# Feature-major FFN tiles in pairs by Strassen's seven block products, on one core of a Trainium2 chip

## The chip, the cores and the metric

The kernel runs on one core of one Trainium2 chip. The metric is the device time of one execution in microseconds (us), lower is better. Three runs of the kernel before the change took 1806.98, 1807.10 and 1807.12 us; the median is 1807.1 us.

A core has five engines that run side by side, each through its own queue of instructions in order: TensorE (PE; its weight loads are shown apart as PEld), VectorE (DVE), ScalarE (ACT), GpSimd (POOL) and SyncE (SP, which here only starts DMAs). TensorE multiplies a stationary block of 128x128 weights with a moving block of up to 512 columns and adds the result up in PSUM (8 banks of 512 float32 for each of the 128 partitions). ACT and DVE take results out of PSUM into SBUF.

## The reference, cut to what matters

512 tokens of width 1024 pass through three blocks. Two are the layers of a transformer, each with attention and a gated feed-forward network:

```python
def swiglu(x, w_in, w_out):                     # w_in 1024 x 5632, w_out 2816 x 1024
    gate, up = jnp.split(x @ w_in, 2, axis=-1)
    return (jax.nn.silu(gate) * up) @ w_out
```

The third has a gated mixer and a feed-forward network with a squared ReLU:

```python
    f = rmsnorm(h, pre_ff_g[l]) @ w_ff1[l]      # 1024 x 4096
    f = jnp.square(jax.nn.relu(f)) @ w_ff2[l]   # 4096 x 1024
```

All is float32. The change touches only the products `x @ w_in` (twice) and `h @ w_ff1` (once).

## The kernel before, in words

**Products in three passes.** Each float32 operand is held as two parts, `hi` (the value as ACT writes it into the type fp32r) and `lo` (the rest, from a subtraction on DVE). A product is hi*hi + hi*lo + lo*hi, three matmuls into one PSUM region (`passes`, L244 to L247).

**Weights.** The list `specs` holds every weight tile of 128x1024 numbers in the order of use. `Weights.load` (L62) starts its DMA into one of 3 raw buffers; `_split` (L77) makes `whi` on ACT (L93) and `wlo` on DVE (L94) into one of 5 pairs of buffers. `done(i)` marks a tile as used up and calls `fill`, which lets the split of tile i+5 follow. So weights are ready up to five tiles ahead.

**The feature-major tiles.** `in_tiles` (L381) runs over the tiles of an input product. One tile is 128 output features for all 512 tokens: 8 blocks of the depth of 1024, each in three passes, so 24 matmuls of 512 columns into one PSUM bank. The first few tiles of a phase (`lead`, 4 or 5) run their first 256 tokens early, while the normalisation of the other tokens is still under way, and so take 24 matmuls of 256 columns for each half. `ffn` (L642) has 22 gate and 22 up tiles in turn: `evac` takes silu of the gate tile (L651) and multiplies the up tile into it (L656). The squared-ReLU phase has 32 tiles, evacuated by L1134 (ACT) and L1135 (DVE).

**The output product.** `out_phase` (L347) then takes the hidden tiles one after another. `splitter` (L634) makes their two parts, `sh` on ACT (L637) and `sl` on DVE (L638), and `Out.__call__` (L320) does 4 token tiles x 2 halves x 3 passes of 512 columns (L333) for each.

**What sets the order.** DMA starts on SP follow the program's order. For the other engines a planner places the instructions when the kernel is built: it goes through them by their place in the program, takes an instruction earlier when its engine is free in the planner's own reckoning and all its inputs and buffers are there, and fixes one order for each engine. A pool's memory can be taken by a later pool once the last reader of the old tiles is done. Semaphores are set by the framework.

Of the kernel before, what the change touches and what calls it, by code (L numbers as in the profile page):

```python
# [10 lines left out]
F32 = mybir.dt.float32  # L11
F32R = mybir.dt.float32r
AF = mybir.ActivationFunctionType
OP = mybir.AluOpType
# [38 lines left out]
class Weights:  # L53


    def __init__(self, nc, raw, pairs, specs, n_raw, n_pairs):
        self.nc, self.raw, self.pairs, self.specs = nc, raw, pairs, specs
        self.n_raw, self.n_pairs = n_raw, n_pairs
        self.loaded, self.split, self.released = 0, 0, 0
        self.r, self.p, self.extra = {}, {}, set()  # L60

    def load(self, parts=0):  # L62
# [11 lines left out]
            return lambda m: self.nc.sync.dma_start(part(v, m), part(src, m))  # L74
        self.nc.sync.dma_start(v, src)

    def _split(self, pool, steps=1, name=None):  # L77
        i = self.split
        while self.loaded <= i:
            self.load()  # L80
        _, (a, b), _ = self.specs[i]
        t = self.r.pop(i)
# [12 lines left out]

        step(range((steps + 1) // 2))
        self.p[i] = tuple(w[:, :a * b].rearrange("p (a b) -> p a b", a=a) for w in (hi, lo))
        self.split += 1
        rest = lambda: step(range((steps + 1) // 2, steps))
        return rest  # L100

    def ahead(self, pool, n, name=None):

        for _ in range(n):
            self.extra.add(self.split)
            self._split(pool, name=name)
        while self.loaded < min(self.split + self.n_raw, len(self.specs)):
            self.load()

    def fill(self, steps=0):  # L110
        end = len(self.specs)
        if steps:
            return self._split(self.pairs, steps)
        while self.split < min(self.released + self.n_pairs + len(self.extra), end):
            self._split(self.pairs)
        while self.loaded < min(self.split + self.n_raw, end):
            self.load()

    def get(self, i):
        return self.p[i]  # L120
# [10 lines left out]
def body(ctx, tc, ins, out, stop=None, dbg=None):  # L131
# [11 lines left out]
    specs, at = [], {}  # L143

    def spec(key, w, r0, nk, c0, n, pad=None):
        at[key] = len(specs)
# [16 lines left out]
    def ffn_specs(l):  # L163
        w = ins["ffn_w_in"][l]
        for f in range(22):
            spec(("fg", l, f), w, 0, 8, 128 * f, 128)
            spec(("fu", l, f), w, 0, 8, FF + 128 * f, 128)
        rows(("fo", l), ins["ffn_w_out"][l], 22)

    ffn_specs(0)  # L170
# [20 lines left out]
    for f in range(32):  # L191
        spec(("f1", f), ins["w_ff1_2"], 0, 8, 128 * f, 128)
    rows("f2", ins["w_ff2_2"], 32)


# [13 lines left out]
    W = Weights(nc, raw, pairs, specs, 3, 5)  # L209

    def load_x(t):
        nc.sync.dma_start(x[t], ins["x"][0, ts(t), :])
# [36 lines left out]
    def bank(*shape):  # L249
        return psum.tile([128, *(shape or (512,))], F32, name="ps")  # L250
# [127 lines left out]
                after(1)  # L378
        finish(3, o.banks[3])

    def in_tiles(keys, evac, lead=0, tails=()):  # L381


        def run(key, p, a, b):
            w = W.get(at[key])
            for k in range(KT):
                passes(p[:, a:b], w, (xh, xl), k == 0, k == KT - 1, (slice(None), k), (slice(None), k, slice(a, b)))

        early = [bank() for _ in keys[:lead]]
        for n, key in enumerate(keys[:lead]):  # L390
            run(key, early[n], 0, 256)
            if n < len(tails):
                for f in tails[n]:
                    f()
        for n, key in enumerate(keys):
            p = early[n] if n < lead else bank()
            run(key, p, 256 if n < lead else 0, 512)
            W.done(at[key])
            evac(n, p)

    def part_project(key, state, part):

# [230 lines left out]
    def splitter(pool, src):  # L633
# [5 lines left out]
            return hi, lo  # L639
        return operand  # L640

    def ffn(l, tails, finish, after):  # L642
        with tc.tile_pool(name="hs", bufs=TAIL[l]) as hs, tc.tile_pool(name="silu", bufs=2) as sp, \
             tc.tile_pool(name="h", bufs=6) as hp:
            h, gate = [], {}

            def evac(n, p):
                f = n // 2
                if n % 2 == 0:
                    gate[f] = sp.tile([128, S], F32, name="gate")  # L650
                    nc.scalar.activation(gate[f], p, AF.Silu)  # L651
                else:
                    if f % 4 == 0:
                        four = hp.tile([128, 4 * S], F32, name="h4")
                        h.extend(four[:, n * S:n * S + S] for n in range(4))
                    nc.vector.tensor_tensor(h[f], p, gate.pop(f), op=OP.mult)  # L656

            keys = [k for f in range(22) for k in (("fg", l, f), ("fu", l, f))]
            in_tiles(keys, evac, 4, tails)
# [471 lines left out]
    h = hp.tile([128, 32, S], F32, name="h2")  # L1131

    def evac_f1(n, p):
        nc.scalar.activation(h[:, n], p, AF.Relu)  # L1134
        nc.vector.tensor_tensor(h[:, n], h[:, n], h[:, n], op=OP.mult)  # L1135

    in_tiles([("f1", f) for f in range(32)], evac_f1, 5, [[], [lambda: after_mix(2)], [], [], [lambda: after_mix(3)]])
    nc.sync.dma_start(gb[:, 0], bcast(ins["post_ff_g_2"], D))

    def finish_ff(t, banks):  # L1140
# [3 lines left out]
    def last_tile(o, ks):  # L1144
# [19 lines left out]
        for k in ks:  # L1164
            o.done(k)

    out_phase(Out("f2", range(32), splitter(hs, [h[:, k] for k in range(32)])), finish_ff, lambda t: None, 4,
              last=last_tile)


# [21 lines left out]
```

## Time and profile before

| | |
|---|---|
| median of 3 runs | 1807.1 us |
| profiled execution | 1812.42 us, of which 1810.6 us from the first to the last instruction |
| TensorE matmul busy | 1773.8 us (98%), 9092 matmuls |
| VectorE busy | 905.7 us (50%) |
| ScalarE busy | 774.7 us (43%) |
| granted TensorE clock | 0.995 of full speed |

The profile is one execution. Busy matmuls overlap in the records (each stands with its whole passage through the array), so the pace of a stream is read from the starts of its matmuls or from the length of a stretch over its count, not from the mean duration of one. "L247" is line 247 of the kernel; names such as `ps<-xh,whi` are the tiles written and read.

### The profile page before, as it was taken

What the parts mean: (1) busy time and instruction counts of PE and PEld (TensorE: products, weight loads), DVE (VectorE), ACT (ScalarE), POOL (GpSimd) and SP (SyncE); (2) the same over time, 40 slices, a digit from 0 to 9 for tenths busy, and PEclk for the clock granted to TensorE, in tenths of its full rate; (3) what the DMA queues carried; (4) which work ended last, traced back from release to release, by engine and by line L of the source; (5) the groups of instructions that cost most, each with busy time, mean ns of one, the idle gap of its engine ahead of it and who ended that gap; (6) DMA issues with size and microseconds to landing.
All of it is one profiled execution on the core that took longest, in us unless ns stands there. A gap on an engine that the chain in (4) does not pass through costs nothing.

```text
span 1810.6 us, 23050 instructions
## 1 busy us (share of the span) xinstructions
PE 1773.8 (98%) x9092; PEld 1499.7 (83%) x9092; DVE 905.7 (50%) x1620; ACT 774.7 (43%) x1341; POOL 69.7 (4%) x125
## 2 busy tenths in 40 slices
PE   8899999999999989999999999999999999999998
PEld 8788788888888878888888888888877898888886
DVE  6888854323234557777633223346456553333333
ACT  6878833222223348878432222233434433223222
POOL 0000000000000020000000000001001100000000
PEclk9999999999999989999999999999999999999999
DMA  6122233333333172222333332342222243333231
GB/s 201 58 59 71 70 128 94 96 102 93 96 126 116 48 228 82 87 83 70 105 105 93 99 99 93 122 136 71 75 77 79 79 117 93 94 104 105 93 104 48
DMA packets 198221, 176.62 MB, mean 98 GB/s; under 512 B 7009, under 2 KB 175137, under 8 KB 198113
## 3 DMA queue, kind: packets, MB, share of 16 engines
q1 hardware_dynamic: 194384, 162.48, 29.5%
q0 software_dynamic: 3152, 10.84, 2.0%
q8 instruction: 71, 1.16, 0.3%
q10 hardware_dynamic: 576, 1.84, 0.3%
q14 instruction: 38, 0.30, 0.1%
HBM read 172.99 MB, written 7.38 MB: 100 GB/s over the span
## 4 chain that ended last, share of the span: by engine, by line
PE 88%; ACT 5%; DVE 4%; issue 1%; DMA 1%; POOL 0%; SPq 0%; DVEq 0%; POOLq 0%; ACTq 0%
PE ps L247 52%; PE ps L333 29%; PE ps L263 1%; PE ps L739 1%; PE ps L751 1%; ACT whi L93 1%; ACT x L500 1%; PE ps L455 1%; DMA wraw<-in_b_w_q 1%; PE ps L456 1%; DVE wlo L94 1%; ACT qk L447 0%; ACT b_e L730 0%; ACT qk L443 0%; PE ps L562 0%
## 5 line engine op out<-in xcount | busy, mean ns | idle before, releaser
L93 ACT ACTIVATE whi<-wraw 128x1024 fp32r<-128x1024 f32 (+1 forms) x278 | 290.4, 1048 | 554.7 <-PE ps L247 457.8
L247 PE MATMUL ps<-xh,whi 128*128 128x512 f32 (+1 forms) x1416 | 518.2, 367 | 1.0 <-ACT xh L265 1.0
L247 PE MATMUL ps<-xl,whi 128*128 128x512 f32 (+1 forms) x1416 | 517.0, 365 | 0.5 <-DVE xl L266 0.3
L247 PE MATMUL ps<-xh,wlo 128*128 128x512 f32 (+1 forms) x1416 | 516.7, 365 | 0.0
L94 DVE TENSOR_TENSOR wlo<-wraw,whi 128x1024 fp32r<-128x1024 f32 (+1 forms) x278 | 336.2, 1213 | 355.3 <-ACT whi L93 350.4
L247 PEld LDWEIGHTS ps<-xh,whi 128*128 128x128 f32 x1416 | 267.2, 189 | 43.4 <-ACT xh L265 2.2
L247 PEld LDWEIGHTS ps<-xl,whi 128*128 128x128 f32 x1416 | 268.2, 189 | 41.7 <-DVE xl L266 1.0
L247 PEld LDWEIGHTS ps<-xh,wlo 128*128 128x128 f32 x1416 | 268.0, 189 | 41.0
L333 PE MATMUL ps<-whi,sh 128*128 128x512 f32 x568 | 176.0, 390 | 0.0
L333 PE MATMUL ps<-wlo,sh 128*128 128x512 f32 x568 | 175.6, 389 | 0.0
L333 PE MATMUL ps<-whi,sl 128*128 128x512 f32 x568 | 175.4, 389 | 0.0
L638 DVE TENSOR_TENSOR sl<-h,sh 128x512 fp32r<-128x512 f32 x76 | 52.6, 691 | 176.5 <-ACT sh L637 176.4
L637 ACT ACTIVATE sh<-h 128x512 fp32r<-128x512 f32 x76 | 47.9, 631 | 211.6 <-PE ps L333 210.7
L247 PE MATMUL ps<-whi,xh 128*128 128x256 f32 (+1 forms) x384 | 125.1, 326 | 0.0
L333 PEld LDWEIGHTS ps<-wlo,sh 128*128 128x128 f32 x568 | 106.6, 188 | 22.3
L333 PEld LDWEIGHTS ps<-whi,sl 128*128 128x128 f32 x568 | 106.6, 188 | 22.1
L333 PEld LDWEIGHTS ps<-whi,sh 128*128 128x128 f32 x568 | 106.3, 188 | 21.8
L247 PE MATMUL ps<-wlo,xh 128*128 128x256 f32 (+1 forms) x384 | 123.1, 321 | 0.0
L247 PE MATMUL ps<-whi,xl 128*128 128x256 f32 (+1 forms) x384 | 123.1, 321 | 0.0
L656 DVE TENSOR_TENSOR h<-ps,gate 128x512 f32<-128x512 f32 x44 | 30.4, 692 | 138.6 <-PE ps L247 137.2
L247 PEld LDWEIGHTS ps<-whi,xh 128*128 128x128 f32 x384 | 73.4, 191 | 6.5 <-issue 1.3
L247 PEld LDWEIGHTS ps<-whi,xl 128*128 128x128 f32 x384 | 73.5, 191 | 5.4
(286 smaller groups left out, 1984.6 us busy)
## 6 DMA issues: line engine op xcount, KB each, us to landing
wraw<-in_ffn_w_in SPq DMA_DIRECT2D x88, 512.0 KB, 3.9
wraw<-in_w_ff SPq DMA_DIRECT2D x64, 512.0 KB, 3.9
wraw<-in_ffn_w_out SPq DMA_DIRECT2D x44, 512.0 KB, 3.3
wraw<-in_a_w_qkv SPq DMA_DIRECT2D x23, 512.0 KB, 3.9
wraw<-in_w_in SPq DMA_DIRECT2D x20, 512.0 KB, 3.7
wraw<-in_kv_w SPq DMA_DIRECT2D x16, 512.0 KB, 4.1
copies<-extd POOLq DMA_DIRECT2D x16, 320.0 KB, 7.4
wraw<-in_a_w_o SPq DMA_DIRECT2D x8, 512.0 KB, 3.3
```

Of the source, the lines that this page charges most:

```text
L93: self.nc.scalar.activation(hi[:, sl], t[:, sl], AF.Copy)
L94: self.nc.vector.tensor_tensor(lo[:, sl], t[:, sl], hi[:, sl].bitcast(F32), op=OP.subtract)
L247: nc.tensor.matmul(ps, lhs[a][lsel], rhs[b][rsel], start=first and n == 0, stop=last and n == 2)
L263: nc.tensor.transpose(p[:, k, :], y[:, ts(4 * c + k)], ident)
L333: nc.tensor.matmul(self.banks[t][c], act[a][:, ts(t)], w[b][:, 0, c * 512:(c + 1) * 512], start=first and n == 0, stop=last and n == 2)
L455: yield lambda: nc.tensor.matmul(p[:, :N], part[m][:, ts(i)], part[2 + m][:, :N], start=True, stop=False)
L456: yield lambda: nc.tensor.matmul(p[:, :N], part[m][:, ts(i)], part[4 + m][:, :N], start=False, stop=True)
L500: nc.scalar.activation(qs[32 * g:32 * g + 32], p[32 * (g ^ 1):32 * (g ^ 1) + 32], AF.Copy)
L637: nc.scalar.activation(hi, src[k], AF.Copy)
L638: nc.vector.tensor_tensor(lo, src[k], hi.bitcast(F32), op=OP.subtract)
L656: nc.vector.tensor_tensor(h[f], p, gate.pop(f), op=OP.mult)
L739: nc.tensor.transpose(p[:, j], e[:, ts(j)], ident)
```

## The change

Of the 60 pairs of feature-major tiles (22 gate/up pairs in each of two layers, 16 pairs of neighbouring tiles in the squared-ReLU phase), 29 are computed by blocks. In the two layers these are the pairs f = 5, 6, 8, 9, 11, 12, 14, 15, 17, 18, 20, 21; in the third phase f = 5, 6, 8, 9, 11. A pair is a product of 256 features x 1024 depth x 512 tokens. Each of the three sizes is halved, and the eight block products become seven, each of 128 features x 512 depth x 256 tokens (4 blocks of depth x 3 passes = 12 matmuls of 256 columns), with sums and differences of blocks on DVE before and after (Winograd's form). A pair takes 4 PSUM banks in place of 2.

The weights of such a pair are four units in place of two: the first raw tile as it is, one half of the second (512 columns), then both raw tiles after four DVE operations of 512 columns in place. The sums of activation blocks (`th`, `tl`) are made once per phase, in 12 steps spread over tiles 4 to 9 (two layers) or 5 to 8 (third phase). They use hidden tiles that are not yet written as scratch, and `gb` (the gains and biases of the normalisation) holds results of pairs. The pool `hs` of `sh` and `sl` is now opened after the pool `blocks` is closed, in its memory. In the third phase the last 8 hidden tiles and `hs2` come after `blocks2` in the same way.

```diff
+FAST = tuple(f for f in range(22) if f >= 5 and f % 3 != 1)
+FAST1 = (5, 6, 8, 9, 11)
...
+    def _source(self, i, part):
+        while self.loaded <= i + (part not in (None, 0)):
+            self.load()
+        if part is None:
+            self.used += 1
+            return self.r.pop(i)[:, :]
+        if part == 0:
+            return self.r[i][:, :]
+        one, two = (self.r[i + n] for n in range(2))
+        (a11, a12), (a21, a22) = ((t[:, :512], t[:, 512:]) for t in (one, two))
+        if part == 1:
+            return a22
+        if part == 2:
+            tt = self.nc.vector.tensor_tensor
+            tt(a22, a21, a22, op=OP.add)
+            tt(a21, a11, a21, op=OP.subtract)
+            tt(a11, a22, a11, op=OP.subtract)
+            tt(a12, a12, a11, op=OP.subtract)
+            return one[:, :]
+        self.used += 2
+        del self.r[i], self.r[i + 1]
+        return two[:, :]
...
+    class Blocks:
+        def __init__(self, f, th, tl, z):
+            quarter = lambda t: t.rearrange("p (a b) -> p a b", b=256)
+            self.f, self.t, self.n = f, (th, tl), 0
+            self.z = [(quarter(gb[:, 0]), quarter(gb[:, 1, :512])), (quarter(z), quarter(gb[:, 1, 512:]))]
+        def steps(self):
+            tt = nc.vector.tensor_tensor
+            f, half = self.f, (slice(0, 256), slice(256, 512))
+            (b11, b12), (b21, b22) = ([f[j][:, :, h] for h in half] for j in range(2))
+            def whole(j, h):
+                sl = (slice(None), slice(4 * j, 4 * j + 4), half[h])
+                tt(f[j][:, :, half[h]], xh[sl].bitcast(F32), xl[sl].bitcast(F32), op=OP.add)
+            def parts(j, h):
+                hi, lo = (t[:, j, :, half[h]] for t in self.t)
+                v = f[j][:, :, half[h]]
+                nc.scalar.activation(hi, v, AF.Copy)
+                tt(lo, v, hi.bitcast(F32), op=OP.subtract)
+            sub = lambda d, a, b: (lambda: tt(d, a, b, op=OP.subtract))
+            return [lambda: whole(0, 0), lambda: whole(0, 1), sub(b11, b12, b11), lambda: whole(1, 1),
+                    lambda: parts(0, 0), sub(b12, b22, b12), lambda: whole(1, 0), sub(b22, b22, b11),
+                    lambda: parts(0, 1), sub(b21, b21, b22), lambda: parts(1, 0), lambda: parts(1, 1)]
+        def __call__(self, key):
+            a, b, c, d = (bank(2, 256) for _ in range(4))
+            z, u = self.z[self.n % 2]
+            self.n += 1
+            def product(part, h, dst, src, j, right):
+                w = W.get(at[key, part])
+                for k in range(4):
+                    sel = (slice(None), 4 * j + k) if src[0] is xh else (slice(None), j, k)
+                    passes(dst, w, src, k == 0, k == 3, (slice(None), 4 * h + k),
+                           (*sel, slice(256 * right, 256 * right + 256)))
+            X, T, tt = (xh, xl), self.t, nc.vector.tensor_tensor
+            product(0, 0, d[:, 0], X, 0, 0)
+            nc.scalar.activation(z[:, 1], d[:, 0], AF.Copy)
+            product(0, 1, a[:, 0], X, 1, 0)
+            W.done(at[key, 0])
+            product(1, 0, c[:, 1], T, 1, 0)
+            W.done(at[key, 1])
+            product(2, 0, a[:, 1], T, 1, 1)
+            tt(z[:, 0:4:3], a, z[:, 1:2].to_broadcast([128, 2, 256]), op=OP.add)
+            product(2, 1, c[:, 0], X, 1, 1)
+            W.done(at[key, 2])
+            product(3, 0, b[:, 1], T, 0, 1)
+            product(3, 1, b[:, 0], T, 0, 0)
+            W.done(at[key, 3])
+            tt(u, b, z[:, 3:4].to_broadcast([128, 2, 256]), op=OP.add)
+            tt(z[:, 1:3], c, u, op=OP.add)
+            tt(z[:, 3], b[:, 0], u[:, 1], op=OP.add)
+            return z
...
     def ffn(l, tails, finish, after):
-        with tc.tile_pool(name="hs", bufs=TAIL[l]) as hs, tc.tile_pool(name="silu", bufs=2) as sp, \
-             tc.tile_pool(name="h", bufs=6) as hp:
...
+                def fast(n, key):
+                    z = blocks(key)
+                    nc.scalar.activation(z[:, 0:2], z[:, 0:2], AF.Silu)
+                    nc.vector.tensor_tensor(h[n // 2].rearrange("p (a b) -> p a b", a=2), z[:, 2:4], z[:, 0:2], op=OP.mult)
+
+                keys = [k for f in range(22) for k in pair_keys(("f", l, f), f in FAST)]
+                in_tiles(keys, evac, 4, tails, fast, side_steps(blocks.steps(), 4, 2))
             load_gb(ins["ln_g"][l, 1], ins["ln_b"][l, 1])
-            out_phase(Out(("fo", l), range(22), splitter(hs, h)), finish, after, TAIL[l],
-                      (SPARE[l], lambda: W.ahead(hp, 1, "h4")))
+            with tc.tile_pool(name="hs", bufs=TAIL[l]) as hs:
+                out_phase(Out(("fo", l), range(22), splitter(hs, h)), finish, after, TAIL[l],
+                          (SPARE[l], lambda: W.ahead(hp, 1, "h4")))
...
+    def fast_f1(n, key):
+        z, to = blocks(key), at_h(n, 2).rearrange("p n (a b) -> p (n a) b", a=2)
+        nc.scalar.activation(to, z[:, 0:4], AF.Relu)
+        nc.scalar.activation(to, to, AF.Square)
```

## Rows read from the trace of the kernel before

**Rows 1.** The page: span; busy time of the engines; granted clock in 40 slices.
```profile
span 1810.6 us, 23050 instructions
PE 1773.8 (98%) x9092; PEld 1499.7 (83%) x9092; DVE 905.7 (50%) x1620; ACT 774.7 (43%) x1341; POOL 69.7 (4%) x125
PEclk9999999999999989999999999999999999999999
```

**Rows 2.** The chain that ended last: start us, length us, what (xmatmuls).
```profile
267.64 5.75 PE ps L247 x48
...
281.14 229.43 PE ps L247 x1056
510.57 107.44 PE ps L333 x474
...
1458.25 8.63 PE ps L247 x72
...
1468.00 161.69 PE ps L247 x768
```

**Rows 3.** Timeline of PE and PEld, layer 0: start, length, instruction.
```profile
267.59 0.28 PE L247 MATMUL ps<-xl,whi 128*128 128x256 f32 x1
...
273.11 0.28 PE L247 MATMUL ps<-xh,wlo 128*128 128x256 f32 x1
...
500.21 0.39 PE L247 MATMUL ps<-xh,whi 128*128 128x512 f32 x1
500.21 0.19 PEld L247 LDWEIGHTS ps<-xl,whi 128*128 128x128 f32 x1
...
509.73 0.39 PE L247 MATMUL ps<-xh,whi 128*128 128x512 f32 x1
```

**Rows 4.** Stretches: length, busy PE, PEld, DVE, ACT, POOL, granted clock, DMA share, GB/s.
```profile
267.60:273.40 5.80, 5.80 (x51) 5.80 (x50) 4.11 (x10) 2.58 (x5) 0.00 (x0) 1.00 0.85 234
402.00:510.60 108.60, 108.60 (x480) 89.96 (x480) 31.31 (x30) 25.86 (x31) 0.00 (x0) 1.00 0.32 97
```

**Rows 5.** Groups by line and shape: busy us, mean ns | idle before, its releaser.
```profile
L93 ACT ACTIVATE whi<-wraw 128x1024 fp32r<-128x1024 f32 x274 | 288.9, 1057 | 554.7 <-PE ps L247 457.8 <-issue 52.1 <-PE ps L333 22.8
L94 DVE TENSOR_TENSOR wlo<-wraw,whi 128x1024 fp32r<-128x1024 f32 x274 | 334.7, 1224 | 355.3 <-ACT whi L93 350.4
L638 DVE TENSOR_TENSOR sl<-h,sh 128x512 fp32r<-128x512 f32 x76 | 52.6, 691 | 176.5 <-ACT sh L637 176.4
L637 ACT ACTIVATE sh<-h 128x512 fp32r<-128x512 f32 x76 | 47.9, 631 | 211.6 <-PE ps L333 210.7 <-DVE h L1135 0.9
L1135 DVE TENSOR_TENSOR h<-h 128x512 f32<-128x512 f32 x32 | 21.9, 684 | 0.0
L656 DVE TENSOR_TENSOR h<-ps,gate 128x512 f32<-128x512 f32 x44 | 30.4, 692 | 138.6 <-PE ps L247 137.2 <-ACT gate L651 1.4
L716 DVE TENSOR_TENSOR v<-ps,v 128x256 fp32r<-128x256 f32 x16 | 6.7, 418 | 4.4 <-ACT v L715 4.3
L651 ACT ACTIVATE gate<-ps 128x512 f32<-128x512 f32 x44 | 25.5, 579 | 0.0
L715 ACT ACTIVATE v<-ps 128x256 fp32r<-128x256 f32 x16 | 6.0, 375 | 6.5 <-PE ps L247 6.4
```

**Rows 6.** Issues of the weights' DMAs: count, KB each, us to landing.
```profile
wraw<-in_ffn_w_in SPq DMA_DIRECT2D x88, 512.0 KB, 3.9
```

**Rows 7.** `sh`: duration min/median/max in ns, first and last start in us.
```profile
L637 ACT ACTIVATE sh<-h x76: 614/632/635, 288.7 to 1776.2; 128x512 fp32r<-128x512 f32 x76
```

**Rows 8.** Timeline at the end of layer 0's input tiles (PE, ACT, DVE).
```profile
510.18 0.39 PE L247 MATMUL ps<-xh,wlo 128*128 128x512 f32 x1
510.38 1.06 ACT L93 ACTIVATE whi<-wraw 128x1024 fp32r<-128x1024 f32 x1 [3.90 <-PE ps L247]
510.41 0.62 PE L333 MATMUL ps<-whi,sh 128*128 128x512 f32 x2
510.68 0.69 DVE L656 TENSOR_TENSOR h<-ps,gate 128x512 f32<-128x512 f32 x1 [3.42 <-PE ps L247]
```

More of the change, by code (lines that the diff above doesn't have):

```diff
@@ L53, with __init__ @@
 class Weights:
-    def __init__(self, nc, raw, pairs, specs, n_raw, n_pairs):
-        self.nc, self.raw, self.pairs, self.specs = nc, raw, pairs, specs
+    def __init__(self, nc, raw, pairs, specs, units, n_raw, n_pairs):
+        self.nc, self.raw, self.pairs, self.specs, self.units = nc, raw, pairs, specs, units
         self.n_raw, self.n_pairs = n_raw, n_pairs
-        self.loaded, self.split, self.released = 0, 0, 0
+        self.loaded, self.used, self.split, self.released = 0, 0, 0, 0
         self.r, self.p, self.extra = {}, {}, set()
@@ L75, in load @@
         self.nc.sync.dma_start(v, src)
-    def _split(self, pool, steps=1, name=None):
[L78 to L82, printed above, removed]
+    def _source(self, i, part):
[20 more added lines that the diff above has]
+        return two[:, :]
+    def _split(self, pool, steps=1, name=None):
+        i, part = self.units[self.split]
+        t = self._source(i, part)
+        (a, b) = (t.shape[1] // 128, 128) if part is not None else self.specs[i][1]
         if name:
@@ L96, in _split @@
         step(range((steps + 1) // 2))
[L97 removed]
+        self.p[self.split] = tuple(w[:, :a * b].rearrange("p (a b) -> p a b", a=a) for w in (hi, lo))
         self.split += 1
@@ L100, in _split, with _loads @@
         return rest
+    def _loads(self):
+        while self.loaded < min(self.used + self.n_raw, len(self.specs)):
+            self.load()
     def ahead(self, pool, n, name=None):
@@ L106, in ahead @@
             self._split(pool, name=name)
[L107 to L108 removed]
+        self._loads()
     def fill(self, steps=0):
[L111 removed]
         if steps:
             return self._split(self.pairs, steps)
[L114 removed]
+        while self.split < min(self.released + self.n_pairs + len(self.extra), len(self.units)):
             self._split(self.pairs)
[L116 to L117 removed]
+        self._loads()
     def get(self, i):
@@ L140, in cols, with spec, spec_pair @@
         return bass.AP(tensor=w.tensor, offset=w.offset + r0 * ld + c0, ap=[[ld, 128], [128 * ld, nk], [1, n]])
-    specs, at = [], {}
-    def spec(key, w, r0, nk, c0, n, pad=None):
-        at[key] = len(specs)
-        specs.append((cols(w, r0, nk, c0, n), (nk, pad or n), n if pad else None))
+    specs, units, at = [], [], {}
+    def spec(key, w, r0, nk, c0, n, pad=None, unit=True):
+        if unit:
+            at[key] = len(units)
+            units.append((len(specs), None))
+        specs.append((cols(w, r0, nk, c0, n), (nk, pad or n), n if pad else None))
+    def spec_pair(key, w, c0, c1, fast):
+        if fast:
+            for part in range(4):
+                at[key, part] = len(units)
+                units.append((len(specs), part))
+        for m, c in enumerate((c0, c1)):
+            spec((key, "one", m), w, 0, 8, c, 128, unit=not fast)
     def rows(key, w, n):
@@ L208, in body @@
     xl = const.tile([128, KT, S], F32R, name="xl")
-    W = Weights(nc, raw, pairs, specs, 3, 5)
+    W = Weights(nc, raw, pairs, specs, units, 3, 5)
     def load_x(t):
@@ L394, in in_tiles @@
                     f()
[L395 to L399, printed above, removed]
+        n = 0
+        for key in keys:
+            if key[-1] == "pair":
+                fast(n, key[0])
+                n += 1
+            else:
+                p = early[n] if n < lead else bank()
+                run(key, p, 256 if n < lead else 0, 512)
+                W.done(at[key])
+                evac(n, p)
+            for f in side.get(n, ()):
+                f()
+            n += 1
@@ new lines, in pair_keys @@
+    def pair_keys(key, fast):
+        return [(key, "pair")] if fast else [(key, "one", m) for m in range(2)]
+    class Blocks:
[47 more added lines that the diff above has]
+            return z
@@ L640, in splitter, with side_steps @@
         return operand
-    def ffn(l, tails, finish, after):
-        with tc.tile_pool(name="hs", bufs=TAIL[l]) as hs, tc.tile_pool(name="silu", bufs=2) as sp, \
-             tc.tile_pool(name="h", bufs=6) as hp:
[L645 to L659, printed above, removed]
+    def side_steps(steps, n, each):
+        side = {}
+        for i, f in enumerate(steps):
+            side.setdefault(n + i // each, []).append(f)
+        return side
@@ new lines, in ffn, with evac @@
+    def ffn(l, tails, finish, after):
+        with tc.tile_pool(name="h", bufs=6) as hp:
+            four = [hp.tile([128, 4 * S], F32, name="h4") for _ in range(6)]
+            h = [t[:, n * S:n * S + S] for t in four for n in range(4)]
+            with tc.tile_pool(name="blocks", bufs=1) as bp:
+                th, tl = (bp.tile([128, PAD + 8 * S], F32R, name=n)[:, PAD:].rearrange("p (j k s) -> p j k s", j=2, k=4)
+                          for n, PAD in (("th", 112), ("tl", 0)))
+                blocks = Blocks([t.rearrange("p (k s) -> p k s", k=4) for t in four[4:6]], th, tl,
+                                bp.tile([128, 2 * S], F32, name="z"))
+                def evac(n, p):
+                    f = n // 2
+                    if n % 2 == 0:
+                        nc.scalar.activation(h[f], p, AF.Silu)
+                    else:
+                        nc.vector.tensor_tensor(h[f], p, h[f], op=OP.mult)
+                def fast(n, key):
[4 more added lines that the diff above has]
+                in_tiles(keys, evac, 4, tails, fast, side_steps(blocks.steps(), 4, 2))
```

32 lines of the change are left out of this document (21 added, 11 removed).

## The prediction

> **What bounds the kernel now.** I read the page first: TensorE is busy for 1773.8 of 1810.6 us at full granted clock in nearly all slices, DVE for half of the span, ACT for less [rows 1]. Busy matmuls overlap in the records, so this share alone proves nothing; the chain of waits does. In layer 0 it runs on PE through 1056 matmuls of the gate and up tiles for 229.43 us, and from there straight into the output product [rows 2]. The reader is to see there that nothing breaks a phase: from its first tile to its end no wait of another engine ends last. The other way round, ACT's splits of weights wait for PE to give a buffer back (457.8 of 554.7 us idle) [rows 5]. So inside these phases the time is the pace of the matmul stream, and DVE and ACT have room: 31.3 and 25.9 us in a stretch of 108.6 us [rows 4].
>
> **What the change takes from PE.** A pair of tiles is 2 x 24 = 48 matmuls of 512 columns. Their pace: from 500.21 to 509.73 us in layer 0 there are 42 of them, 0.2267 us each [rows 3]. 48 x 0.2267 = 10.88 us. A pair by blocks is 7 products x 12 = 84 matmuls of 256 columns. The kernel before has such a stream, in the early halves of the first tiles: 48 in 5.75 us and 72 in 8.63 us [rows 2], and start to start 46 in 5.52 us [rows 3], so 0.1198 us each. 84 x 0.1198 = 10.06 us. A matmul of half the columns thus costs 0.528 of the whole one: of the 12.5% that seven products for eight would give, 7.5% is left. The gain is 0.82 us a pair, 29 x 0.82 = 23.8 us.
>
> The stream of 256 columns is shown for 8.63 us at a stretch, and in a stretch where DVE was busy for 4.11 of 5.8 us and DMA for 0.85 of it [rows 4], which is about the company that it gets in the change. I take it to hold for 20 us on end.
>
> A rule of the Trainium skill speaks against this. The rows say first: one LDWEIGHTS takes 0.19 us [rows 3], longer than the 0.1198 us from one 256-column matmul to the next, so loads overlap with matmuls of the same rows of the array. "TensorE: Matmul & The Clock Gate", Part 3, "The mechanism", says in my words that a weight load overlaps with a running matmul only where the row groups differ; all of these use the whole array, so each load would stand in line. This case's trace disagrees, and the measurement decides. What the rule would give is the second rival.
>
> **What it adds, and what hides it.** DVE, for one pair by blocks: three splits of 1024 columns at 1.224 and one of 512 at 0.691, four sums of 512 on raw weights at 0.684 (as L1135, both operands in SBUF), three sums of 512 out of PSUM at 0.692 (as L656), one of 256 at 0.418 (as L716), and the last multiplication at 0.684: 3.67 + 0.69 + 2.74 + 2.08 + 0.42 + 0.68 = 10.28 us [rows 5]. The sums with an operand repeated for both halves are not in the trace; two operations of 256 (0.84) bound them above and one of 256 (0.42) below, and I take 0.69, the row of the same size. ACT has 3 x 1.057 + 0.63 + 0.375 + 0.58 = 4.76 us. So during one such pair DVE would need 10.28 us against 10.06 us of PE: that is the point to watch. The two layers run two such pairs and one of the old kind in turn. The old kind costs DVE 2 x 1.224 + 0.69 = 3.14 us. Over three pairs: DVE 23.7 us, PE 2 x 10.06 + 10.88 = 31.0 us. DVE is at 76%, and what is late after two pairs is caught up in the third, if there is enough store of ready weights.
>
> The store: a unit is split when the one five places before is used up. Take two block pairs A and B, time 0 at A's first matmul. A's units end at 2.9, 4.3, 7.2 and 10.1 us (24, 12, 24, 24 matmuls). B's third unit, the one with the four sums, starts after A's second: DVE 2.74 from about 5.2 (B's second split stands before it), ACT 1.06, DVE 1.22, ready at about 10.2. PE wants it at 10.06 + 2.88 + 1.44 = 14.4. In the same way the others have 4 us and more in hand. The 3 raw buffers hold too: a DMA lands 3.9 us after issue [rows 6], B's second tile goes out when A's last unit is split, about 5 us ahead of A's start, and is wanted at 2.9. PSUM: a pair takes 4 of 8 banks, its results leave within some 5 us, the banks come round after 10. I cost all this at nothing; the cover is PE's own stream.
>
> The 12 steps for the activation sums are 12 x 1.224 = 14.7 us of DVE and 4.2 us of ACT per phase. Beside tiles 4 to 9 of a layer (6 x 5.44 = 32.7 us) DVE has 6 x 1.224 + 3 x 0.69 = 9.4 us else, so 24.1 of 32.7 fit. In the third phase they lie beside tiles 5 to 8, with a square per tile: 5 x (1.224 + 0.684) + 14.7 + 2.7 for the first pair's weight sums = 26.9 of 27.2 us up to tile 9, tight. The planner brings work forward where an engine is free (the first `sh` runs at 288.7 us, 222 us before its use [rows 7]), and the tiles before have room. Bounds per phase: 0, and 2.5 us when the last two steps wait behind tile 9's work (a split, a multiplication, 1.06 + 1.22 of their own). I take 0.5, near the lower end, for that same reason: 1.5 us for three.
>
> **What stands on the path.** `hs` now lies in the memory of `th` and `tl`. Before, `sh` was made far ahead, and the output product started without a gap at 510.41 [rows 8]. After, the first `sh` must wait until the last matmul of pair 21 has read `th`; pair 21 is a block pair in both layers. Then ACT takes 0.63 (and ahead of it a weight split of 1.06, as ACT in fact starts one in that moment at 510.38 [rows 8]), and DVE has two or three sums of the pair (0.69, 0.69, 0.42) and that split's `wlo` (1.22) before `sl` (0.69). PE gets 4 matmuls (0.91 us) between needing `sh` and needing `sl`. Lower bound: 0.2 for the last result to drain + 0.63 + semaphores 0.07 = 0.9 us. Upper: 0.2 + 0.69 + 0.69 + 1.22 + 0.42 + 0.69 + 0.69 - 0.91 = 3.7 us. I take 3.0, nearer to the upper end, because rows show the split going first there; two layers, 6.0 us. The third phase's last 8 tiles are of the old kind, so its `hs2` is free long before.
>
> `load_gb` on SP waits for pair 21's results as well, some 3 us; the loads queued behind it are for tiles five units ahead (27 us), so nobody waits.
>
> **Sum.** -23.8 + 6.0 + 1.5 = -16.3 us. The profiled execution took 1812.4 us, so 1796.1 for one like it; the median is 5.3 us lower than the profiled one, and 1807.1 - 16.3 = 1790.8 us.
>
> **Rivals.** First, *DVE holds PE up, slower.* The engine takes its queue in order. (The Trainium skill, "TensorE: Matmul & The Clock Gate", "Architectural detail", says that ACT and DVE are strictly first in, first out; nothing in this sum goes by that page.) If the planner's own durations make it put the sums of A out of PSUM before B's weight sums, these start only when A has ended: 10.06 + 1.8 + 0.58 + 0.68 = 13.1, + 2.74 + 1.06 + 1.22 = 18.1 against 14.4 wanted, a wait of about 3.5 us in each second pair of two. There are 6 + 6 + 2 = 14 such places: +49 us, 1839.8 us. It decides from 16.3 / 14 = 1.2 us a place. For it: DVE at 102% within a block pair. Against it: the text of the kernel has the weight sums first, and raw tiles are there early.
>
> Second, *the weight loads set the pace.* If 256-column matmuls went at the 0.19 us of a LDWEIGHTS, a pair would take 84 x 0.19 = 16.0 us, 29 x 5.1 = 148 us more: 1807.1 + 148 + 7.5 = 1963 us. Against it stand the 48 and 72 matmuls at 0.1198. This is the rule named above, with its own small chance.
>
> Third, *small waits eat part of the gain.* With seven products and four units a pair there are more places to wait. At 0.3 us a pair the result is 1790.8 + 8.7 = 1799.5; at 0.56 us a pair there is no gain and the time stays at 1807. For it: the tight DVE. Against it: in the trace, groups of 12 or 24 matmuls follow each other without a gap.
>
> Fourth, *the gain without its price*: 0.9 us at each boundary and no wait at the start gives 1807.1 - 23.8 + 1.8 = 1785.1 us.
>
> **Chances.** My forecast, 1787 to 1795: 0.58. The gain without its price: 0.16. Part of it eaten, 1795 to 1803.5: 0.14. No gain: 0.03. DVE holds PE up: 0.08. Weight loads: 0.01. A change of 0.2%, 3.6 us, is about what a measurement here can tell from none: faster 0.58 + 0.16 + 0.14 = 0.88, same 0.03, slower 0.09. The range goes from 1783.5, just under the best sum, to 1799.5, the third rival's time; the worst ends of all bounds (3.7 x 2 and 2.5 x 3) give 1807.1 - 23.8 + 14.9 = 1798.2 and lie inside.
>
> **What would show it.** Starts of 256-column matmuls 0.1198 us apart in the block pairs, 10.06 us a pair, and 29 x 84 = 2436 of them in the place of 29 x 48 = 1392 of 512 columns. DVE about 75% busy in the layers' input phases. At both boundaries to the output product, PE idle for 1 to 4 us, released by ACT's `sh` and then DVE's `sl`; none in the third phase. Waits of PE for `whi` or `wlo` of a third unit would make the first rival true, a pace above 0.125 us the second; waits of PE for PSUM banks or for `th` at each pair, the third.

## The result, and the profile after

The changed kernel took 1791.64 us (median of 4 runs, 1790.75 to 1794.19), the kernel before 1807.11 us beside it. The ratio is 0.9914, with a 95% interval of 0.9902 to 0.9927: faster by 0.9%. The forecast was 1790.8 us, in a range of 1783.5 to 1799.5. The sum came out, but its two largest terms were wrong, and by about the same amount in opposite directions. That is what the rest of this document is about.

The page of the changed kernel, answering to [rows 1]: busy us, share, instructions.

```profile
span 1790.0 us, 25646 instructions
PE 1745.7 (98%) x10136; PEld 1524.4 (85%) x10136; DVE 1127.7 (63%) x1936; ACT 848.6 (47%) x1440; POOL 70.9 (4%) x125
```

PE has 1044 matmuls more (29 x 36) and DVE 222 us more, yet the span is shorter: DVE's work found its place beside PE.

The chain that ended last, answering to [rows 2]: start, length, what. L285 is now the line of the input tiles, L371 that of the output product.

```profile
267.37 5.75 PE ps L285 x48
...
280.87 199.36 PE ps L285 x1343
...
502.13 109.71 PE ps L371 x474
...
1117.49 106.50 PE ps L371 x462
...
1452.93 156.17 PE ps L285 x948
```

Compare landmarks. From the first early half to the first matmul of the output product it was 510.57 - 267.64 = 242.9 us, and is 502.13 - 267.37 = 234.8. The output product's first stretch of 474 was 107.44 and is 109.71 us. The third phase (768 matmuls before, 948 now) went from 161.69 to 156.17 us. Between the chain's 199.36 us and the output product lie over 20 us of other pieces, though PE was busy for most of it: the chain left PE because something other than PE ended last, just before the output product.

Stage by stage the change gave -8.2 and -8.4 us in the two layers' input tiles (first early half to output product), +2.3 and +2.0 us in the work behind them (up to the first tiles of what follows), -5.5 us in the third phase: -17.8 us. The spans of the two profiles differ by 20.6 us. 2.5 of the other 2.8 us lie in the attention of layer 1, which the change does not touch; a second profile of the kernel before (below) shows that they belong to that one execution.

The pace of the matmuls, answering to [rows 3]: timeline of PE in pair 21 of layer 0.

```profile
487.77 0.28 PE L285 MATMUL ps<-xh,whi 128*128 128x256 f32 x1
...
489.81 0.28 PE L285 MATMUL ps<-xh,wlo 128*128 128x256 f32 x1
...
490.51 0.28 PE L285 MATMUL ps<-th,wlo 128*128 128x256 f32 x1
...
492.55 0.28 PE L285 MATMUL ps<-th,wlo 128*128 128x256 f32 x1
```

From start to start, 17 matmuls of `xh` and `xl` take 2.04 us, 0.120 us each, as predicted; 18 of `th` and `tl` take 2.04 us, 0.113 (0.114 over whole pairs). The products with sums of activations are quicker than the 256-column matmuls of [rows 3].

A stretch of three pairs, two by blocks and one as before, answering to [rows 4].

```profile
336.00:367.00 31.00, 31.00 (x223) 29.11 (x222) 22.91 (x31) 11.97 (x17) 0.00 (x0) 1.00 0.37 103
```

DVE is busy for 22.9 of 31.0 us (74%; predicted 76%), PE without a break.

The end of layer 0's input tiles, answering to [rows 8]: first PE, then DVE, then ACT.

```profile
496.71 0.28 PE L285 MATMUL ps<-th,wlo 128*128 128x256 f32 x1
502.13 1.22 PE L371 MATMUL ps<-whi,sh 128*128 128x512 f32 x2 [5.14 <-ACT sh L751]
503.15 1.05 PE L371 MATMUL ps<-wlo,sh 128*128 128x512 f32 x2
...
505.71 0.91 PE L371 MATMUL ps<-wlo,sh 128*128 128x512 f32 x2
506.45 0.63 PE L371 MATMUL ps<-whi,sl 128*128 128x512 f32 x2
```
```profile
497.68 0.68 DVE L510 TENSOR_TENSOR gb<-ps,z 128x512 f32<-128x512 f32 x1
498.40 0.69 DVE L511 TENSOR_TENSOR z<-ps,gb 128x512 f32<-128x512 f32 x1
499.01 1.22 DVE L121 TENSOR_TENSOR wlo<-wraw,whi 128x1024 fp32r<-128x1024 f32 x1
500.14 0.42 DVE L512 TENSOR_TENSOR z<-ps,gb 128x256 f32<-128x256 f32 x1
500.66 0.69 DVE L783 TENSOR_TENSOR h<-z 128x512 f32<-128x512 f32 x1
```
```profile
497.58 1.06 ACT L120 ACTIVATE whi<-wraw 128x1024 fp32r<-128x1024 f32 x1 [1.55 <-DMA wraw<-in_ffn_w_out]
499.18 0.63 ACT L782 ACTIVATE z<-z 128x512 f32<-128x512 f32 x1 [0.55 <-DVE z L511]
501.44 3.23 ACT L751 ACTIVATE sh<-h 128x512 fp32r<-128x512 f32 x6 [1.63 <-DVE h L783]
```

PE stands still for 5.1 us. ACT stood ready for 1.63 us before the first `sh`, and what released it was DVE's last multiplication of pair 21 (L783), which reads `z`. Then PE comes back at about half pace: six matmuls of 512 columns from 503.15 to 505.71, 0.427 us each.

```profile
496.80:502.10 5.30, 0.19 (x2) 0.00 (x0) 4.41 (x6) 2.34 (x4) 0.00 (x0) 0.75 0.81 237
502.10:506.50 4.40, 4.37 (x11) 3.47 (x12) 3.70 (x6) 2.57 (x5) 0.00 (x0) 0.52 0.75 303
```

The granted clock stands behind the busy times of the five engines: 0.75 for the stretch of the standstill, in which it fell, and 0.52 for the 4.4 us behind it, about the lower of the two levels (1.2 GHz). Layer 1 shows the same: 4.9 us of standstill, a low clock behind it, and 1.8 us more in the output product's first stretch (106.50 against 104.72). First the matmul behind the standstill, then the stretch:

```profile
1117.49 1.22 PE L371 MATMUL ps<-whi,sh 128*128 128x512 f32 x2 [4.93 <-ACT sh L751]
1117.40:1121.00 3.60, 3.51 (x9) 2.79 (x10) 3.53 (x6) 3.16 (x7) 0.00 (x0) 0.54 0.90 350
```

The idle times count from the end of the last matmul's record. Against the pace of the stream, start to start, the two standstills cost 5.3 and 5.1 us, together 10.39 us. With the slow stretches behind them the two ends cost 10.39 + 2.27 + 1.78 = 14.4 us.

### The profile page after: what moved, and what is told of

Its sections match the earlier page's. It is cut to its first block, busy times and chain, and to the rows that moved or that the text cites. A ratio compares the mean times of both kernels' runs of the same rounds, so it can differ in the third digit from the quotient of the medians.

```text
span 1790.0 us, 25646 instructions
## 1 busy us (share of the span) xinstructions
PE 1745.7 (98%) x10136; PEld 1524.4 (85%) x10136; DVE 1127.7 (63%) x1936; ACT 848.6 (47%) x1440; POOL 70.9 (4%) x125
## 4 chain that ended last, share of the span: by engine, by line
PE 86%; ACT 6%; DVE 5%; DMA 2%; issue 1%; POOL 0%; SPq 0%; DVEq 0%; POOLq 0%; ACTq 0%
PE ps L285 50%; PE ps L371 30%; ACT whi L120 1%; PE ps L301 1%; ACT x L614 1%; DVE wlo L121 1%; DMA wraw<-in_kv_w 1%; PE ps L879 1%; PE ps L867 1%; PE ps L569 1%; PE ps L570 1%; DMA wraw<-in_ffn_w_out 1%; ACT qk L561 1%; ACT qk L557 0%; PE ps L676 0%
## 5 line engine op out<-in xcount | busy, mean ns | idle before, releaser
L120 ACT ACTIVATE whi<-wraw 128x1024 fp32r<-128x1024 f32 (+2 forms) x336 | 337.6, 1011 | 432.4 <-PE ps L285 164.6
L121 DVE TENSOR_TENSOR wlo<-wraw,whi 128x1024 fp32r<-128x1024 f32 (+2 forms) x336 | 390.1, 1167 | 212.1 <-ACT whi L120 204.9
L285 PE MATMUL ps<-xh,whi 128*128 128x256 f32 (+1 forms) x1300 | 435.9, 337 | 1.0 <-ACT xh L303 1.0
L285 PE MATMUL ps<-xl,whi 128*128 128x256 f32 (+1 forms) x1300 | 435.1, 335 | 0.5 <-DVE xl L304 0.3
L285 PE MATMUL ps<-xh,wlo 128*128 128x256 f32 (+1 forms) x1300 | 435.0, 335 | 0.0
L285 PEld LDWEIGHTS ps<-xh,whi 128*128 128x128 f32 x1300 | 246.4, 190 | 25.1 <-ACT xh L303 2.0
L285 PEld LDWEIGHTS ps<-xl,whi 128*128 128x128 f32 x1300 | 247.4, 190 | 23.6 <-DVE xl L304 1.0
L285 PEld LDWEIGHTS ps<-xh,wlo 128*128 128x128 f32 x1300 | 247.4, 190 | 23.4
L371 PE MATMUL ps<-whi,sh 128*128 128x512 f32 x568 | 177.8, 393 | 10.1 <-ACT sh L751 10.1
L371 PE MATMUL ps<-wlo,sh 128*128 128x512 f32 x568 | 176.8, 392 | 0.0
L371 PE MATMUL ps<-whi,sl 128*128 128x512 f32 x568 | 176.5, 391 | 0.0
L371 PEld LDWEIGHTS ps<-whi,sh 128*128 128x128 f32 x568 | 107.2, 190 | 32.4 <-ACT sh L751 10.5
L285 PE MATMUL ps<-th,whi 128*128 128x256 f32 x464 | 128.8, 278 | 0.0
L285 PE MATMUL ps<-tl,whi 128*128 128x256 f32 x464 | 128.5, 277 | 0.0
L285 PE MATMUL ps<-th,wlo 128*128 128x256 f32 x464 | 128.3, 277 | 0.0
L371 PEld LDWEIGHTS ps<-wlo,sh 128*128 128x128 f32 x568 | 107.5, 189 | 22.5
L371 PEld LDWEIGHTS ps<-whi,sl 128*128 128x128 f32 x568 | 107.3, 189 | 22.5
L285 PE MATMUL ps<-whi,xh 128*128 128x256 f32 (+1 forms) x384 | 125.1, 326 | 0.0
L285 PE MATMUL ps<-wlo,xh 128*128 128x256 f32 (+1 forms) x384 | 123.2, 321 | 0.0
L285 PE MATMUL ps<-whi,xl 128*128 128x256 f32 (+1 forms) x384 | 123.2, 321 | 0.0
```

The lines of the kernel that those rows point to most:

```text
L285: nc.tensor.matmul(ps, lhs[a][lsel], rhs[b][rsel], start=first and n == 0, stop=last and n == 2)
L371: nc.tensor.matmul(self.banks[t][c], act[a][:, ts(t)], w[b][:, 0, c * 512:(c + 1) * 512], start=first and n == 0, stop=last and n == 2)
```

## The experiments

All ran beside the kernel before, which took 1808.3 to 1808.6 us there, 1.2 to 1.5 us more than beside the changed kernel. Ratios and stages of the profiles are safer to compare than times of different runs.

**Where the moving tile starts.** `th` is preceded by a padding of 448 bytes (112 numbers), in a line of the diff that is not among those shown ahead. No trace shows an address: the starts named here are worked out from the sizes of the tiles in the kernel. With the padding, `th` and `tl` start on a multiple of 128 bytes; `xh`, `xl` and the split weights start 64 bytes beside one.

*th64*, the padding away (in the third phase, `th2`, too):
```diff
-                          for n, PAD in (("th", 112), ("tl", 0)))
+                          for n, PAD in (("th", 0), ("tl", 0)))
```


> The changed kernel with the padding ahead of th taken away (112 numbers to 0, in all three phases), so that th and tl start 64 bytes off a multiple of 128 in SBUF, as xh and xl do; nothing else. In the changed kernel the matmuls that stream th or tl come 0.1142 us apart and those that stream xh or xl 0.1197 us. Theory A (where the moving operand starts sets the pace): all 256-column matmuls go to 0.1197 us, 48 of the 84 of a pair get 5.5 ns slower, 29 x 48 x 0.0055 = 7.7 us more, 1799.3 us. Theory B (th and tl are quick for another reason, such as their place or their size): pace of th stays at 0.114, time 1791.6 within 1.5.

1799.92 us (ratio to before 0.9949, 0.9933 to 0.9966), 8.3 us more than the changed kernel; by stages, from the long stretch of the input tiles to the output product in the two layers and in the third phase, 3.2 + 3.4 + 1.6 = 8.2 us more. The pace of `th` is that of `xh`, start to start:

```profile
482.34 0.28 PE L285 MATMUL ps<-th,whi 128*128 128x256 f32 x1
...
483.78 0.28 PE L285 MATMUL ps<-th,whi 128*128 128x256 f32 x1
```

12 matmuls in 1.44 us, 0.120 each. So about 8 of the 15.5 us that the changed kernel gained on the kernel before hang on this padding. Theory B is out; whether it is the start as such (A) or the start against the weights (C), this run can't tell.

*all128* and *before128*, every tile on a multiple of 128 bytes:
```diff
-    mhalf = const.tile([128, 8], F32, name="mhalf")
+    mhalf = const.tile([128, 24], F32, name="mhalf")
```
(and in all128 the padding of `th` away)

> The changed kernel with mhalf 24 numbers wide in place of 8, which moves every later SBUF tile by 64 bytes onto a multiple of 128, and without the padding ahead of th (so th and tl stay on such a multiple). Nothing that is computed changes. Theory A (a moving operand that starts on a multiple of 128 bytes is quicker): the 256-column matmuls of xh and xl go from 0.1197 to 0.114 us, and the 512-column ones, if the price is one per matmul, from 0.2267 to about 0.221; some 8700 such matmuls stand on the path, 5.5 ns each is 48 us, 1744 us (1735 to 1755). Theory C (th is quick because it starts at another offset than the weights that are loaded at the same time): weights and moving tiles again share one offset, so all go at 0.1197, 1799 us.

> The kernel before with mhalf 24 numbers wide in place of 8: all later SBUF tiles 64 bytes further on, onto multiples of 128; nothing else. Theory A: 512-column matmuls from 0.2267 to about 0.221 us and 256-column ones from 0.1198 to 0.114, about 7900 matmuls on the path at 5.5 ns, 43 us less, 1764 us (1755 to 1775). Theory C: no change, 1807 us. With the run of the changed kernel so aligned it tells what the seven products are worth when both kernels have the quicker pace: then a pair costs 48 x 0.221 = 10.6 against 84 x 0.114 = 9.6 us, 29 us for 29 pairs less the two waits of 7.3 us at the ends of the input phases, so 15 to 20 us between the two.

1800.06 us (0.9954, 0.9938 to 0.9971) and 1808.73 us (1.0006, 0.9995 to 1.0017): nothing gained on th64 and on the kernel before, all 256-column matmuls at 0.120 us. Theory A, my first, is dead. Not where a tile starts counts, but where it starts against the weights loaded beside it.

*off* and *before_off*, weights moved by 64 bytes against everything else:
```diff
+    for pool in (raw, small):
+        nc.gpsimd.memset(pool.tile([128, 16], F32, name="gap", bufs=1), 0.0)
```
(and in off the padding of `th` away)

> The changed kernel with 64 bytes left free in SBUF ahead of the raw weights and 64 behind the split ones, and the padding ahead of th taken away: the split weights start on a multiple of 128 bytes, and xh, xl, th, tl, sh and sl all 64 bytes beside one. Theory C (a matmul is quicker where the weights that are loaded beside it and the moving tile start 64 bytes apart, modulo 128): all 256-column matmuls at 0.114 us, the 512-column ones at about 0.221, some 8700 on the path at 5.6 ns less than 0.1197 and 0.2267 beside the 1392 of th and tl that have it already, about 7300 x 5.6 ns = 41 us less than 1791.6: 1751 (1742 to 1762). Theory C2 (only 256-column matmuls gain, since a load of weights is over long before a 512-column one ends): the 1044 of xh and xl in the block pairs and some 900 others, 10 us, 1781.

> The kernel before with the same 64 bytes ahead of the raw weights and behind the split ones; nothing else. Theory C: about 7900 matmuls on the path at 5.6 ns less, 44 us, 1764 us (1755 to 1775). Theory C2: only its some 1900 256-column matmuls gain, 10 us, 1798. The difference to the changed kernel with the same offsets is what the seven products are worth when both have the quicker pace.

1812.77 us (1.0025, 1.0016 to 1.0035) and 1834.68 us (1.0150, 1.0135 to 1.0165): slower, where both theories had said faster. The chain of before_off against [rows 2] shows why.

```profile
895.82 5.66 PE ps L249 x48
...
909.13 235.18 PE ps L249 x1056
...
1481.18 165.24 PE ps L249 x768
1646.41 179.22 PE ps L335 x768
```

48 matmuls of 256 columns take 5.66 us in place of 5.75, but the phase with its 960 of 512 columns takes 235.2 in place of 229.4 us. Starting 64 bytes apart helps the narrow matmul (0.1198 to 0.118) and hurts the wide one (0.2267 to 0.233). The two runs also say what the seven products are worth where the weights are moved in both kernels: 1834.68 - 1812.77 = 21.9 us, against 1808.73 - 1800.06 = 8.7 us where every start is on a multiple of 128.

*x0* and *no21_x0*, weights where they were and every moving tile of the input phases on a multiple of 128 (no21 is below):
```diff
+    nc.gpsimd.memset(raw.tile([128, 16], F32, name="gap", bufs=1), 0.0)
...
-    mhalf = const.tile([128, 8], F32, name="mhalf")
+    mhalf = const.tile([128, 24], F32, name="mhalf")
```


> The changed kernel with mhalf 24 numbers wide and 64 bytes left free ahead of the raw weights: xh, xl, th and tl start on a multiple of 128 bytes, the split weights 64 bytes beside one, as only th and tl did against the weights in the changed kernel; sh and sl keep the weights' offset. Runs so far: weights at 64 and moving tile at 0 (modulo 128) 0.1142 us per 256 columns; both at 64 or both at 0 0.1197; weights at 0 and moving at 64 0.1175, and 0.234 per 512 columns. Theory E (the pair weights 64, moving 0 is quick for either width): 684 x 3 = 2052 matmuls of 256 columns and 616 x 3 = 1848 of 512 at 5.6 ns less, 22 us, 1770 (1766 to 1774). Theory F (whatever sets the two apart by 64 is quick at 256 columns and slow at 512): 11.5 us less and 1848 x 7 ns = 13 us more, 1793 (1790 to 1796).

> Both together: pair 21 as before in both layers, and the offsets of x0. Theory E: 1779.6 - 22 = 1758 (1754 to 1763). Theory F: 1781 (1778 to 1784).

1796.43 us (0.9932, 0.9917 to 0.9948) and 1781.38 us (0.9843, 0.9821 to 0.9864). Theory F: the gain on narrow matmuls is paid back on wide ones. But the two layers, with the same instructions, differ:

```profile
280.34 202.42 PE ps L286 x1343
...
899.78 199.02 PE ps L286 x1343
```

*no21_x128*, the same distance of 64 at another place (`mhalf` 56 wide, same gap ahead of the raw weights, pair 21 as before):

> The run no21 with mhalf 56 numbers wide and 64 bytes left free ahead of the raw weights: modulo 256 the split weights start at 192 and xh, xl, th and tl at 128, as only th and tl did against the weights in the changed kernel, where 256 columns took 0.1142 us; in x0 the same two stood at 64 and 0 and 256 columns took 0.1175, 512 columns 0.233. Theory I (the place modulo 256 decides, not only the distance of 64): all 256-column matmuls at 0.1142 us, and if 512 columns gain too (0.221) some 22 us less than no21, 1758 (1754 to 1764); if they lose as in x0 (0.233), 11 us less and 12 us more, 1780 (1777 to 1783), with the pace of 256 columns telling. Theory J (the place modulo 256 doesn't matter): paces as in x0, 0.1175 and 0.233, 1781 (1778 to 1785).

1783.22 us (0.9869, 0.9847 to 0.9891): no gain on no21. In the pairs the narrow matmuls come 0.113 us apart and the wide ones 0.233, the paces of theory I's second branch. But the early halves keep 0.118 (48 in 5.66 us), and layer 1 of no21_x0 had the quick pace without the move. First layer 1 of no21_x0, then layer 0 of this run:

```profile
891.46 217.11 PE ps L286 x1452
280.07 217.11 PE ps L286 x1452
```

So the run does not decide between theories I and J.

**The standstill at the ends.**

*zapart*, `z` in a pool of its own, so that closing `blocks` frees `th` and `tl` alone:
```diff
-        with tc.tile_pool(name="h", bufs=6) as hp:
+        with tc.tile_pool(name="h", bufs=6) as hp, tc.tile_pool(name="zp", bufs=1) as zp:
...
-                                bp.tile([128, 2 * S], F32, name="z"))
+                                zp.tile([128, 2 * S], F32, name="z"))
```


> The changed kernel with z of the two layers in a pool of its own below blocks that stays open beside hs, so that closing blocks frees th and tl alone. In the changed kernel TensorE stands still for 5.1 and 4.9 us at the two ends of the input tiles, until the first sh, and sh waited for the last multiplication of pair 21 (DVE), which reads z. Theory D (the pool's memory is taken as one, so sh waits for z's last reader): now sh waits for the last matmul alone, the gap falls to 1 to 3 us and the half clock behind it (2.1 us a time) may go: 1782 to 1788 us. Rival (sh waits because ACT or DVE come to it late, behind splits of weights that waited for their DMA): the gap stays at 4 us or more and the time at 1789 to 1793.

1783.54 us (0.9865, 0.9848 to 0.9882). PE and ACT at the end of layer 0's input tiles:

```profile
496.42 0.28 PE L285 MATMUL ps<-th,wlo 128*128 128x256 f32 x1
498.50 0.73 PE L371 MATMUL ps<-whi,sh 128*128 128x512 f32 x2 [1.80 <-ACT sh L751]
```
```profile
496.87 1.06 ACT L120 ACTIVATE whi<-wraw 128x1024 fp32r<-128x1024 f32 x1 [1.17 <-DMA wraw<-in_ffn_w_out]
497.84 1.14 ACT L751 ACTIVATE sh<-h 128x512 fp32r<-128x512 f32 x2
498.88 0.64 ACT L782 ACTIVATE z<-z 128x512 f32<-128x512 f32 x1
```

The standstill falls to 1.8 us, and `sh` now follows the last matmul with one split of weights (1.06 us) ahead of it. Theory D: the wait was for `z`. Layer 1 stands still for 1.75 us. In layer 0 the clock still fell, after PE had come back, and the 474 matmuls take 109.36 us; in layer 1 it stayed up, and the 462 take 105.06 us against 104.72. The stretches behind the two standstills:

```profile
498.50:502.90 4.40, 4.40 (x13) 3.45 (x14) 4.40 (x8) 3.09 (x6) 0.00 (x0) 0.63 0.77 223
1110.70:1115.00 4.30, 4.30 (x19) 3.53 (x20) 4.30 (x8) 3.55 (x7) 0.00 (x0) 1.00 0.71 218
```

*no21*, pair 21 of both layers as before:
```diff
-FAST = tuple(f for f in range(22) if f >= 5 and f % 3 != 1)
+FAST = tuple(f for f in range(22) if 5 <= f < 21 and f % 3 != 1)
```


> The changed kernel with pair 21 of both layers computed as before (27 block pairs instead of 29). Then th, tl and z are done with one pair (10.9 us) before the output product begins. Theory D: sh is made meanwhile, no gap and no half clock at the two ends; 2 x (5.1 + 2.1) = 14.5 us less, 2 x 1.1 us more for the two pairs: 1779 us (1777 to 1782). Rival (the gap comes from late weights of the output product): most of it stays, 1788 or more.

1779.61 us (0.9841, 0.9825 to 0.9857), faster than both kernels, with two block pairs fewer. The chain:

```profile
280.78 217.26 PE ps L285 x1452
498.04 107.44 PE ps L371 x474
...
894.91 217.26 PE ps L285 x1452
1112.18 104.72 PE ps L371 x462
```

One unbroken stretch, no half clock behind it (107.44 and 104.72 as in [rows 2] and in the second layer before). It also measures a pair by itself: (229.43 - 217.26) / 11 = 1.106 us gained by each of 11; the third phase says (161.69 - 156.17) / 5 = 1.104.

**DVE's room.** *every*, all pairs from 5 to 21 by blocks:
```diff
-FAST = tuple(f for f in range(22) if f >= 5 and f % 3 != 1)
+FAST = tuple(f for f in range(22) if f >= 5)
```


> The changed kernel with every pair from f = 5 to 21 of the two layers computed by blocks: 17 a layer in place of 12, no old pair between. TensorE then needs 9.77 us a pair and DVE 10.28 without a break. Theory G (the old pairs between are DVE's time to catch up): DVE falls back by half a microsecond a pair and more where it waits on ACT in its queue, the lead of some 4 us is used up, and TensorE waits for weight units in the later part of each phase; of the 2 x 5 x 1.11 = 11 us that TensorE saves at most half is left: 1785 to 1800. Theory H (DVE's queue has room even so): 1780.5 (1778 to 1783), with the two gaps at the ends as before.

1815.36 us (1.0038, 1.0025 to 1.0051): slower than the kernel before. From 360.8 us on PE waits in nearly every pair of layer 0, where `whi` or `wlo` of the third unit is due. Waits of ACT and SP between 300 and 500 us (total us, times, longest), then PE, then ACT:

```profile
ACT whi L120 <- DVE wraw L100: 50.4, 13, 4.2
ACT whi L120 <- DMA wraw<-in_ffn_w_in: 43.7, 14, 5.1
SPq L78 <- DVE wlo L121: 187.6, 33, 15.6
```
```profile
419.11 0.38 PE L285 MATMUL ps<-th,wlo 128*128 128x256 f32 x1 [0.66 <-DVE wlo L121]
...
440.63 0.38 PE L285 MATMUL ps<-th,whi 128*128 128x256 f32 x1 [0.76 <-ACT whi L120]
...
441.92 0.39 PE L285 MATMUL ps<-th,wlo 128*128 128x256 f32 x1 [0.79 <-DVE wlo L121]
```
```profile
435.14 0.63 ACT L120 ACTIVATE whi<-wraw 128x512 fp32r<-128x512 f32 x1 [3.78 <-DMA wraw<-in_ffn_w_in]
439.52 2.95 ACT L120 ACTIVATE whi<-wraw 128x1024 fp32r<-128x1024 f32 x3 [3.75 <-DVE wraw L100]
```

Theory G has the place right (PE waits for units of weights) and the size wrong: it said 1785 to 1800. Its reason, DVE that falls back, is at most a part of it, for DVE is not simply full: from 420 to 460 us it was busy for 34.7 of 40 us. What the trace shows turning is a ring through the 3 raw buffers. A pair's second tile lands (435.1), its half is split (0.63 and 0.69), the four sums follow (436.5 to 439.4), then three splits; only then are two raw buffers free for the next pair's loads (SP, which starts them, waits for `wlo`), 4 to 5 us to landing. From the third unit's `wlo` at 419.11 to that of the next pair but one at 441.92 this is 11.4 us a pair, where PE needs 9.8. That it is the raw buffers and not DVE's queue order was not tried apart.

**The kernel before, once more.** *before_again*, unchanged:

> The kernel before, once more and unchanged, for a second profile of it. The first profiled execution took 1812.4 us where the median is 1807.1, and between 632 and 670 us, at the start of layer 1's attention, its TensorE waited for weights' DMAs. If the 5.3 us are that execution's own, this one takes about 1807 us and the stretch from the first tile of layer 1's attention to the first input tile of layer 1's network is about 5 us shorter than the 259.6 us there; if they are what a profile costs, it takes 1812 again.

1808.2 us. Its chain gives 229.41 and 229.42 us for the two stretches of 1056 and 161.69 for the third, as in the first profile, and 255.9 us for the layer between the two networks, where the first profile had 259.6. So that execution's attention of layer 1 was 4 us late by itself. Against this second profile the changed kernel's span is 1806.4 - 1790.0 = 16.4 us shorter, close to the 15.5 us between the medians. The stages gave 17.8; in the changed kernel's profile that layer took 257.1 us, 1.2 more than here.

## Why the prediction was right, and where it was not

**What bounds the kernel.** Right. PE's stream set the input phases before and after; only where it broke did anything else matter.

**What the change takes from PE: 23.8 us predicted, 32.0 measured.** The term was mis-sized. It used one pace, 0.1198 us, for all 84 matmuls. 36 of them have it, the 48 that stream `th` and `tl` take 0.114, a pair takes 9.78 us in place of 10.06, and 29 x 1.105 = 32.0 us. The padding stood in the diff as `PAD` and I read over it. With it taken away the pace and the price are the predicted ones: th64 is 1799.9 us, and 1808.5 (the kernel before beside it) - 23.8 + 14.4 gives 1799.1.

**What hides the added work: nothing predicted for the pairs, nothing measured.** DVE's sum was right (74% for 76%), and no unit was late. The first rival (DVE holds PE up, 0.08) did not come, but *every* shows that its place was the right one: without the old pairs between, the third unit is late in most pairs, and the kernel is slower than before. The old pairs are not leftovers: with them between, nothing is late. That the ring of raw buffers is what catches up there is read from the trace of *every* and was not tried apart.

**The sums at the start of a phase: 1.5 us predicted, none measured.** PE runs through from 280.87 us to the end of the tiles; the planner had the steps done in time.

**What stands on the path: 6.0 us predicted, 14.4 measured.** This step failed. "The first `sh` must wait until the last matmul of pair 21 has read `th`" was wrong in what it waited for. It waited for the last reader of `z`, another tile of the closed pool: three sums, a split and a multiplication on DVE later. *zapart* takes that away, and what is left is the predicted working: a split of weights of 1.06 us, then `sh`, 1.8 us of standstill. And there was no term for the clock, which fell with the standstill; the stretches behind took 2.3 and 1.8 us more.

**The sum.** -32.0 + 14.4 = -17.6 us against the stages' -17.8, and against -16.3 predicted. The time hit by luck: 8.2 us too little gain met 8.4 us too little loss at the ends, and what is left is the 1.5 us at the starts that did not come. *no21* takes the loss away; by the same terms 1791.6 - 14.4 + 2 x 1.1 = 1779.4 us, and it took 1779.61.

**Weight loads.** The rival by which loads set the pace (0.01) is out: 0.12 us from matmul to matmul for 20 us on end, with loads of 0.19 us each.

## What to carry to other kernels

Seven products for eight paid here because the narrow matmul cost 0.53 of the wide one and other engines had room; both numbers were in the trace beforehand. When a pool's memory is handed on, ask for the last reader of every tile in it, not of the one whose place is taken, and let the last piece of a phase be one that needs none of it. When a forecast hits, check its terms by stage: two errors of 8 us made this one look good.

## What the runs showed of the hardware that was not expected

The pace of a matmul depends on where the moving tile starts in SBUF against the weights. With equal starts modulo 128 bytes it was 0.120 us for 256 columns and 0.2267 for 512, with both on a multiple of 128 (all128, before128) as with both 64 bytes beside one (th64, the kernel before). With starts 64 bytes apart, 256 columns took 0.113 to 0.118 and 512 columns 0.233. So narrow matmuls gain by the distance and wide ones lose, and giving it to all input tiles was no better than giving it to `th` and `tl` alone (x0 against the changed kernel, no21_x128 against no21). The changed kernel gives it to `th` and `tl` alone, which are only streamed 256 wide. What sets the figure between 0.113 and 0.118 stays open: it differed between two layers with the same instructions (202.42 and 199.02 us in x0), and between the early halves and the pairs of one phase (0.118 and 0.113 us in no21_x128). Why the distance acts at all no run shows.

With a standstill of 5 us the granted clock went to its lower level at both ends of the changed kernel (0.52 and 0.54 in the stretch behind), with one of 1.8 us at one of two (zapart, 0.63 and 1.00). The price came behind the standstill, in slower matmuls: 0.427 us for 512 columns in place of 0.2267.
